# A mixture-of-experts stage whose experts are taken in the order of their token counts, with three of them held in one operand tile instead of two

## The chip, the cores and the metric

The kernel runs on one core of one Trainium2 chip. Its time is the device time of one execution in microseconds, and it is stated as the median of several runs. The five engines of a core are TensorE (PE, with its weight loads PEld), VectorE (DVE), ScalarE (ACT), GpSimd (POOL) and SyncE (SP, which here issues the DMAs).

## The reference

Two layers of a diffusion backbone with 256 latent tokens and 256 context tokens, model width 1024. The change is in the last stage, the mixture of experts of the second layer. A router picks for each of the 256 tokens two of eight experts; each expert is a SwiGLU of hidden width 3584:

```python
def _swiglu(h, w1, w3, w2):
    return (jax.nn.silu(h @ w1) * (h @ w3)) @ w2

def _moe(h, w_router, w1, w3, w2):
    logits = (h @ w_router).astype(F32)
    top_v, top_i = lax.top_k(logits, TOP_K)
    top_w = jax.nn.softmax(top_v, axis=-1)
    gates = jnp.sum(jax.nn.one_hot(top_i, N_EXPERTS, dtype=F32) * top_w[..., None], axis=-2).astype(h.dtype)
    out = jnp.zeros_like(h)
    for e in range(N_EXPERTS):
        out = out + gates[..., e:e + 1] * _swiglu(h, w1[e], w3[e], w2[e])
    return out
```

So there are 512 pairs of token and expert. Which expert gets how many depends on the data. `setup_inputs` draws all arrays from a key (`seed=0` by default) and then multiplies some of the parameters by fixed factors. The weights of the eight experts are 352 MB in single precision.

## The kernel before

**Precision.** A product of single precision is made of three products of rounded operands: x and w are each split into a high part and the remainder (`xeh`, `xel` of the tokens; `whi`, `wlo` of the weights), and `mm3` (L244) adds high by high, high by low and low by high in PSUM. ACT writes the high part of a weight tile (L215), DVE the low part (L222). A weight tile is 128 x 2048 values, 1 MB in memory.

**Routing.** `route` (L1445) makes for each half of the tokens the two choices, the gates, and in `pos1` each token's place among its expert's tokens, counted from 1 (0 where the expert is not chosen). L1491 to L1495 count the tokens of each expert and keep the greatest count in `cnt_i`.

**Experts.** `experts` (L1635) goes through the experts 0 to 7 in this order, each in four blocks of hidden columns (`FT`: three of 1024, one of 512). For a block, `up` (L1535) makes the products with w1 and w3 (PSUM tiles `eh`), `mid` (L1600) takes silu times product (`esil`), transposes it on PE (`eT`) and splits it into `ehi` and `elo`; `down` (L1551) of the block before stands between them and adds to the PSUM tiles `ey`. Per expert 42 weight tiles come in, 28 for w1 and w3 and 14 for w2.

**Gather and scatter.** `gather` (L1569) collects the tokens of two experts at once, 128 places for each: a one-hot matrix `ohr` from `pos1`, products with it (`xg`, 256 columns), an affine step on ACT (`xe`), and the split into `xeh` and `xel` on DVE. It is called ahead of expert 0 and in the third block of every second expert. `scatter` (L1620) multiplies the result by the gate row (`ye`), splits it (`yel`, on POOL except for the last expert), brings it back to token places with `ohT` (`es`) and adds it to `macc`.

**More than 128 tokens.** Behind the last expert `finish` (L1666) makes the layer norm and writes the output. Then every engine reads `cnt_i` into a register, and if the greatest count is over 128 all eight experts run once more for the places from 129 on, and `finish` too:

```python
    cv = nc.values_load(cnt_i[0:1, 0:1])
    with tc.If(cv > P):
        experts(P)
        finish()
```

**Order and buffers.** A scheduler places the instructions of each engine; within an engine they run in that order. Weight tiles land in eight buffers (`eraw`, L1521: four and one of `rp`, three of `mr`) and are split into three pairs of `whi` and `wlo` (pool `wq`, `NW` = 3). SP issues all loads in one queue, and each waits for its buffer, that is for the DVE instruction which read it last.

Of the kernel before, what the change touches and what calls it, by code (L numbers as in the profile page):

```python
# [9 lines left out]
F32 = mybir.dt.float32  # L10
# [7 lines left out]
P = 128  # L18
# [20 lines left out]
NMP = 0  # L39
NW = 3  # L40
D = 1024
# [20 lines left out]
def shape_tables():  # L62
# [40 lines left out]
    for h in (0, 16):  # L103
        for j in range(8):
# [10 lines left out]
    t["k_iota"] = np.tile(np.arange(1, 257)[None, :], (P, 1)) * 1.0  # L115
    t["k_cst"] = np.concatenate([t.pop("k_ident"), np.moveaxis(t.pop("k_cum"), 0, 1).reshape(P, -1),
                                 np.moveaxis(t.pop("k_mask"), 0, 1).reshape(P, -1), t.pop("k_bd"), t.pop("k_perm"),
                                 t.pop("k_tri"), t.pop("k_iota")], axis=1)
# [46 lines left out]
def tile_backbone(ctx: ExitStack, tc: tile.TileContext, A: dict, out: bass.AP, dbg=None, upto=99):  # L165
# [1214 lines left out]
    iot = const([P, 256], "iotk")  # L1380
    nc.sync.dma_start(iot, A["k_cst"][:, 1064:1320])
# [52 lines left out]
    cnt_i = keep([1, 1], "cnti", I32)  # L1434
# [9 lines left out]
    raws = {}  # L1444

# [47 lines left out]
    cm = until_experts([1, 1], "cmax")  # L1493
    V.tensor_reduce(cm, cps[0:1, 0:NE], axis=AX.X, op=ALU.max)
    cpy(cnt_i, cm)  # L1495
# [38 lines left out]

    def up(st, key, t):  # L1535
        e, (f0, w_) = st["e"], FT[t]
        ps = [bank("eh", "b") for _ in range(w_ // 512)]
        n = 2048 // w_
        for c0 in range(0, KC, n):
            raw = eraw(key, None).rearrange("p (c f) -> p c f", f=w_)  # L1540
            wload(raw, A[key][0, e, P * c0:P * (c0 + n), f0:f0 + w_].rearrange("(c p) f -> p c f", p=P))
            w = wsplit(raw)
            for k in range(n):
                c = c0 + k
                x = [v[:, c, st["sl"]] for v in st["x"]]
                for hf, acc in enumerate(ps):
                    sl = slice(512 * hf, 512 * hf + 512)
                    mm3(acc, x, (w[0][:, k, sl], w[1][:, k, sl]), c == 0, c == KC - 1)
        return ps

    def down(st, t):  # L1551
        e, (f0, w_) = st["e"], FT[t]
        if t == 0:
            st["y"] = [bank("ey", "a") for _ in range(2)]
        hi, lo = st["h"][t]
        for j2 in range(w_ // 256):

            raw = eraw("moe_w2", None).rearrange("p (c f) -> p c f", f=D)
            r0 = f0 + 256 * j2
            wload(raw, A["moe_w2"][0, e, r0:r0 + 256, :].rearrange("(p c) f -> p c f", c=2))  # L1560
            w = wsplit(raw)
            for c in range(2):
                i = 2 * j2 + c
                for hf in range(2):
                    sl = slice(512 * hf, 512 * hf + 512)
                    mm3(st["y"][hf], (hi[:, i], lo[:, i]), (w[0][:, c, sl], w[1][:, c, sl]),
                        t == 0 and i == 0, t == len(FT) - 1 and i == w_ // P - 1)

    def gather(e0, s0):  # L1569

        ohr = kp_.tile([P, 2, 256], F32R, name=nm("ohr"), tag="ohr", bufs=1)
        ohT = kp_.tile([P, 4, P], F32R, name=nm("ohT"), tag="ohT", bufs=2)
        for b in range(2):
            for j in range(2):
                ts(ohr[:, b, P * j:P * j + P], iot[:, s0:s0 + P], pos1[:, b, e0 + j:e0 + j + 1], ALU.is_equal)
        xeh = mp.tile([P, KC, 256], F32R, name=nm("xeh"), tag="xeh", bufs=2)
        xel = mp.tile([P, KC, 256], F32R, name=nm("xel"), tag="xel", bufs=2)
        for q in range(KC // 2):
            ps = bank("xg", "a", [P, 2, 256])
            xe = mp.tile([P, 2, 256], F32, name=nm("xe"), tag="xe", bufs=2)  # L1580
            for i in range(2):
                c = 2 * q + i
                for b in range(2):
                    sl = slice(P * c, P * c + P)
                    mm(ps[:, i], xhi[:, b, sl], ohr[:, b], b == 0 and i == 0, False, skip_group_check=True)
                    mm(ps[:, i], xlo[:, b, sl], ohr[:, b], False, b == 1 and i == 1, skip_group_check=True)
            for i in range(2):
                c = 2 * q + i
                act(xe[:, i], ps[:, i], AF.Identity, bias=kg[:, 1, c:c + 1], scale=kg[:, 0, c:c + 1])
            sl = slice(2 * q, 2 * q + 2)  # L1590
            split(xeh[:, sl], xel[:, sl], xe, "v")
        tps = bank("ohT", "a", [P, 4, P])
        for j in range(2):
            for b in range(2):
                PE.transpose(tps[:, 2 * j + b], ohr[:, b, P * j:P * j + P].bitcast(F32), ident)
# [125 lines left out]
```

## Time and profile before

| | |
|---|---|
| median of 3 runs | 1998.88 us (1998.78 to 2006.72) |
| the profiled execution | 1999.65 us, of it span 1997.9 us |
| PE busy | 96% of the span |
| DVE, ACT, POOL busy | 70%, 53%, 14% |
| DMA, mean over the span | 247 GB/s |
| first matmul of an expert; last | 995.06 us; 1976.53 us |
| DMA between 1050 and 1950 us | 362 GB/s, the 16 DMA engines 98% busy |

The experts fill the second half of the span. The profiled execution's own time stands 0.77 us over the median. The matmuls are pipelined, so PE's busy time says that it always had one under way, not how fast they followed each other; that is read from their start times. A weight tile's way is SP, DMA, ACT, DVE, PE, and each buffer goes back up the same way; so the first of these engines that can't keep up sets the pace of all.

### The profile page before, as it was taken

How to read it: one execution, taken by the hardware profiler on the slowest of the kernel's cores; microseconds unless marked ns; L12 is line 12 of the kernel's file. 1: busy time of each engine (PE TensorE's matmuls, PEld its weight loads, DVE VectorE, ACT ScalarE, POOL GpSimd, SP SyncE). 2: the span in 40 equal slices, each digit the busy share in tenths (PEclk: the TensorE clock that was granted, in tenths of full speed). 3: DMA queues.
4: the chain of work that ended last, by engine and by line, in shares of the span. 5: the costliest groups of instructions: out<-in, count | busy, mean ns of one | idle time of the engine just before them, and what ended most of it. 6: DMA issues, size and time to landing. Idle time of an engine off the chain costs nothing.

```text
span 1997.9 us, 24418 instructions
## 1 busy us (share of the span) xinstructions
PE 1923.3 (96%) x9615; PEld 1530.2 (77%) x9615; DVE 1400.3 (70%) x1457; ACT 1060.0 (53%) x1057; POOL 273.1 (14%) x235
## 2 busy tenths in 40 slices
PE   6999999899999998999899999999999999999996
PEld 3786467788888887957688888888888888888884
DVE  4653455644333446446789899989889898898986
ACT  3541234332222224325477777777776777777773
POOL 2221220250211226121000000101001010010101
PEclk9999999999999998999899999999999999999998
DMA  9515553413232434365489999999999999999992
GB/s 305 187 69 184 222 197 100 158 64 106 89 109 66 134 113 134 121 243 190 165 305 385 378 348 353 348 369 373 361 346 345 379 364 369 343 349 370 361 377 94
DMA packets 161866, 493.18 MB, mean 247 GB/s; under 512 B 12123, under 2 KB 52928, under 8 KB 141264
## 3 DMA queue, kind: packets, MB, share of 16 engines
q1 hardware_dynamic: 161744, 491.55, 68.1%
q8 instruction: 77, 1.26, 0.3%
q14 instruction: 45, 0.37, 0.1%
HBM read 486.77 MB, written 4.74 MB: 246 GB/s over the span
## 4 chain that ended last, share of the span: by engine, by line
PE 88%; DVE 6%; ACT 1%; POOL 1%; issue 1%; DVEq 0%; ACTq 0%; POOLq 0%
PE eh L234 29%; PE pf L234 17%; PE ey L234 13%; PE w L234 6%; PE wo L234 3%; DVE wlo L222 2%; PE gemv L234 2%; PE pt L234 2%; PE sm L234 2%; PE om L234 1%; PE eT L1615 1%; PE U L234 1%; PE yv L234 1%; PE oa L234 1%; POOL yel L222 1%; PE pT L1080 1%
## 5 line engine op out<-in xcount | busy, mean ns | idle before, releaser
L222 DVE TENSOR_TENSOR wlo<-moe_w,whi 128x2048 fp32r<-128x2048 f32 x336 | 769.0, 2312 | 82.5 <-ACT whi L215 81.6
L215 ACT ACTIVATE whi<-moe_w 128x2048 fp32r<-128x2048 f32 x336 | 644.8, 1921 | 208.9 <-PE eh L234 117.6
L234 PE MATMUL eh<-whi,xel 128*128 128x512 f32 x896 | 349.8, 391 | 1.1 <-DVE xel L222 1.1
L234 PE MATMUL eh<-wlo,xeh 128*128 128x512 f32 x896 | 350.0, 391 | 0.0
L234 PE MATMUL eh<-whi,xeh 128*128 128x512 f32 x896 | 319.1, 391 | 1.9 <-DVE xeh L219 1.9
L234 PE MATMUL pf<-hhi,whi 128*128 128x512 f32 (+2 forms) x560 | 210.1, 379 | 4.8 <-ACT hhi L211 2.3
L234 PE MATMUL pf<-hlo,whi 128*128 128x512 f32 (+2 forms) x560 | 211.5, 378 | 2.1 <-DVE hlo L222 2.0
L234 PE MATMUL pf<-hhi,wlo 128*128 128x512 f32 (+2 forms) x560 | 211.0, 377 | 0.1
L234 PEld LDWEIGHTS eh<-whi,xeh 128*128 128x128 f32 x896 | 168.6, 189 | 37.0 <-DVE xeh L219 2.1
L234 PEld LDWEIGHTS eh<-whi,xel 128*128 128x128 f32 x896 | 168.9, 189 | 36.5 <-DVE xel L222 1.6
L234 PEld LDWEIGHTS eh<-wlo,xeh 128*128 128x128 f32 x896 | 168.8, 188 | 35.3 <-DVE wlo L222 0.2
L234 PE MATMUL ey<-wlo,ehi 128*128 128x512 f32 x448 | 177.9, 397 | 1.3 <-DVE wlo L222 1.3
L234 PE MATMUL ey<-whi,elo 128*128 128x512 f32 x448 | 174.8, 390 | 0.6 <-DVE elo L222 0.6
L234 PE MATMUL ey<-whi,ehi 128*128 128x512 f32 x448 | 157.0, 390 | 0.5 <-ACT ehi L215 0.5
L222 POOL TENSOR_TENSOR yel<-ye,yeh 128x512 fp32r<-128x512 f32 x14 | 38.8, 2770 | 866.1 <-ACT yeh L215 859.4
L215 ACT ACTIVATE whi<-ffn_w 128x1024 fp32r<-128x1024 f32 x44 | 46.7, 1062 | 174.0 <-PE w L234 94.1
L234 PEld LDWEIGHTS pf<-hhi,whi 128*128 128x128 f32 (+1 forms) x560 | 106.2, 191 | 26.9 <-ACT hhi L211 2.6
L234 PEld LDWEIGHTS pf<-hlo,whi 128*128 128x128 f32 (+1 forms) x560 | 106.6, 190 | 24.1 <-DVE hlo L222 3.2
L234 PEld LDWEIGHTS pf<-hhi,wlo 128*128 128x128 f32 (+1 forms) x560 | 106.4, 190 | 20.2 <-issue 1.6
L222 DVE TENSOR_TENSOR wlo<-ffn_w,whi 128x1024 fp32r<-128x1024 f32 x40 | 52.7, 1318 | 73.4 <-ACT whi L215 72.6
L234 PEld LDWEIGHTS ey<-wlo,ehi 128*128 128x128 f32 x448 | 84.4, 188 | 19.8 <-DVE wlo L222 3.4
L234 PEld LDWEIGHTS ey<-whi,ehi 128*128 128x128 f32 x448 | 84.0, 188 | 18.5 <-ACT ehi L215 0.9
(345 smaller groups left out, 2774.9 us busy)
## 6 DMA issues: line engine op xcount, KB each, us to landing
moe_w<-in_moe_w_dram SPq DMA_DIRECT2D x336, 1024.0 KB
wm<-in_w_mod_dram SPq DMA_DIRECT2D x48, 1024.0 KB
ffn_w<-in_ffn_w_dram SPq DMA_DIRECT2D x22, 1024.0 KB
wi<-in_w_in_dram SPq DMA_DIRECT2D x14, 1024.0 KB
w<-in_ffn_w_dram SPq DMA_DIRECT2D x10, 1024.0 KB
wo<-in_w_out_dram SPq DMA_DIRECT2D x8, 1024.0 KB
wmla<-in_p_mla_dram SPq DMA_DIRECT2D x10, 256.0 KB
gate<-grd SPq DMA_DIRECT2D x10, 256.0 KB
```

The lines of the kernel that those rows point to most:

```text
L215: S.activation(o, i, AF.Copy)
L222: (eng or V).tensor_tensor(out=o, in0=a, in1=b, op=op)
L234: PE.matmul(o, l, r, start=start, stop=stop, **kw)
L1080: PE.transpose(pt[:, P * q:P * q + P], pr[:, P * q:P * q + P], ident)
L1615: PE.transpose(ps[:, P * i:P * i + P], s4[:, j2, c], ident)
```

## The change

- A list of slots: `CAPS` gives the places of each slot (128 or 64), `RANKS` which rank by token count it takes. Slot 0 is always expert 0 with 128 places (its key is set to -1, so it has rank 0), so that its loads need no register. The other seven are ranked by their counts; ranks 1, 2 and 3 go to the slots 1, 3 and 7, which have 64 places, the others to slots with 128.
- `order_experts` (new) works out ranks, the experts' numbers by slot (`idx_i`), places and gates by slot (`poss`, `gatess`), and `over_i`, the greatest of count minus places over all slots.
- Loads of the slots 1 to 7 take the expert's number from a register of SP (`expert_at`).
- A slot of 64 places holds the high parts of its tokens in columns 0 to 63 and the low parts in 64 to 127 of one tile. `mmx` then makes two products, with `whi` and with `wlo`; the two halves of rows are added in `mid` by a product with `fold` (two identity matrices, one above the other), which takes the place of the transposes, and after `down` by the scatter, whose one-hot matrix has the places twice.
- `gather` is called once for each slot, with 128 or 64 columns.
- Behind `finish`, the eight slots run once more, with 128 places each, if `over_i` is over 0 (before: if the greatest count was over 128).
- One more buffer for weight tiles (`NMP` = 1).

```diff
-NMP = 0
+NMP = 1
+CAPS = (128, 64, 128, 64, 128, 128, 128, 64)
+RANKS = (0, 1, 4, 2, 5, 6, 7, 3)
...
+    E0 = 0
+    def order_experts():
...
+        key, rank, cs, ov = (v[:, i] for i in range(4))
+        stt(key, cnt_f, float(NE), iot[:, 0:NE], ALU.mult, ALU.add)
+        V.memset(key[:, E0:E0 + 1], -1.0)
+        sq = [P, NE, NE]
+        tt(pm, key[:, :, None].to_broadcast(sq), key[:, None, :].to_broadcast(sq), ALU.is_gt)
+        V.tensor_reduce(rank, pm, axis=AX.X, op=ALU.add)
+        tt(pm, iot[:, 256:264, None].to_broadcast(sq), rank[:, None, :].to_broadcast(sq), ALU.is_equal)
+        tt(n8[:, 0], pm, iot[:, None, 0:NE].to_broadcast(sq), ALU.mult)
+        tt(n8[:, 1], pm, cnt_f[:, None, :].to_broadcast(sq), ALU.mult)
+        V.tensor_reduce(v[:, 2:4], n8, axis=AX.X, op=ALU.add)
+        ts(idx_i, cs[0:1], -1.0, ALU.add)
+        tt(ov, ov, iot[:, 264:272], ALU.subtract)
+        V.tensor_reduce(cs[:, 0:1], ov, axis=AX.X, op=ALU.max)
+        cpy(over_i, cs[0:1, 0:1])
+        for src, dst in ((pos1, poss), (gates, gatess)):
+            for b in range(2):
+                tt(n8[:, b], pm, src[:, b, None, :].to_broadcast(sq), ALU.mult)
+            V.tensor_reduce(dst, n8, axis=AX.X, op=ALU.add)
...
+    def mmx(acc, x, w, first, last):
+        if len(x) == 2:
+            mm3(acc, x, w, first, last)
+        else:
+            mm(acc, x[0], w[0], first, False)
+            mm(acc, x[0], w[1], False, last)
...
+        if len(st["x"]) == 1:
+            s3 = mp.tile([P, 1024], F32, name=nm("es3"), tag="es3")
+            pt = [bank("eT", "a", [P, 8, 64]) for _ in range(2)]
+            for hf in range(n // 512):
+                sh = slice(512 * hf, 512 * hf + 512)
+                for o, src, dst in ((s, p1, pt[0]), (s3, p3, pt[1])):
+                    cpy(o[:, sh], src[hf], "s")
+                    o4 = o[:, sh].rearrange("p (j q c) -> p j c q", j=2, c=2)
+                    for i in range(4):
+                        mm(dst[:, 4 * hf + i], o4[:, i // 2, i % 2], fold, hf == 0 and i == 0,
+                           hf == n // 512 - 1 and i == 3, skip_group_check=True)
+            m = n // P
+            sil = mp.tile([P, 8, 64], F32, name=nm("esl"), tag="esl")
+            act(sil[:, 0:m], pt[0][:, 0:m], AF.Silu)
+            tt(sil[:, 0:m], pt[1][:, 0:m], sil[:, 0:m], ALU.mult)
+            split(hi[:, 0:m, 0:64], hi[:, 0:m, 64:128], sil[:, 0:m])
+            st["h"][t] = (hi,)
+            return
...
+    def expert_at(s):
+        rv = nc.values_load(idx_i[0:1, s:s + 1], engines=(mybir.EngineType.SP,), min_val=0, max_val=NE - 1,
...
+        return bass.ds(rv, 1)
...
-                if t == 2 and e % 2 == 1 and e + 1 < NE:
-                    sts += gather(e + 1, s0)
+                if t == 2 and s + 1 < NE:
+                    nxt = get(s + 1)
...
-    experts(0, True)
+    experts(poss, CAPS, True)
...
-    cv = nc.values_load(cnt_i[0:1, 0:1])
-    with tc.If(cv > P):
-        experts(P)
+    cv = nc.values_load(over_i[0:1, 0:1])
+    with tc.If(cv > 0):
+        pos2 = kp_.tile([P, 2, NE], F32, name="pos2", tag="pos2")
+        for b in range(2):
+            tt(pos2[:, b], poss[:, b], iot[:, 264:272], ALU.subtract)
+        experts(pos2, (P,) * NE)
         finish()
```

**PE, two chunks of an expert's `up`**, in the second expert taken (a chunk is one 128-row piece of the weights; `eh` are the sums, `xeh` and `xel` the tokens). Before:

```order
L234 MATMUL eh_8741<-whi_8763,xeh_7858 128x512
L234 MATMUL eh_8742<-whi_8763,xeh_7858 128x512
L234 MATMUL eh_8741<-wlo_8764,xeh_7858 128x512
L234 MATMUL eh_8741<-whi_8763,xel_7859 128x512
L234 MATMUL eh_8742<-wlo_8764,xeh_7858 128x512
L234 MATMUL eh_8742<-whi_8763,xel_7859 128x512
L234 MATMUL eh_8741<-whi_8763,xeh_7858 128x512
L234 MATMUL eh_8741<-wlo_8764,xeh_7858 128x512
L234 MATMUL eh_8741<-whi_8763,xel_7859 128x512
L234 MATMUL eh_8742<-whi_8763,xeh_7858 128x512
L234 MATMUL eh_8742<-wlo_8764,xeh_7858 128x512
L234 MATMUL eh_8742<-whi_8763,xel_7859 128x512
```

Now, in slot 1, which has 64 places:

```order
L239 MATMUL eh_8814<-whi_8832,xeh_8603 128x512
L239 MATMUL eh_8815<-whi_8832,xeh_8603 128x512
L239 MATMUL eh_8814<-wlo_8833,xeh_8603 128x512
L239 MATMUL eh_8815<-wlo_8833,xeh_8603 128x512
L239 MATMUL eh_8814<-whi_8832,xeh_8603 128x512
L239 MATMUL eh_8814<-wlo_8833,xeh_8603 128x512
L239 MATMUL eh_8815<-whi_8832,xeh_8603 128x512
L239 MATMUL eh_8815<-wlo_8833,xeh_8603 128x512
```

Each pair of `whi` and `wlo` now meets one operand, `xeh`, twice where it met `xeh` twice and `xel` once.

**SP, from the loads of the first expert to those of the second.** Before:

```order
L319 DMA moe_w_1797_8693<-in_moe_w_dram 128x2048
L319 DMA moe_w_1800_8711<-in_moe_w_dram 128x2048
L319 DMA moe_w_1809_8743<-in_moe_w_dram 128x2x1024
L319 DMA moe_w_1812_8761<-in_moe_w_dram 128x2x1024
L319 DMA moe_w_1815_8779<-in_moe_w_dram 128x2x1024
```

Now:

```order
L324 DMA moe_w_1804_8784<-in_moe_w_dram 128x2048
L1698 TENSOR_LOAD idxi
L324 ISA
L324 DMA moe_w_1813_8816<-in_moe_w_dram 128x2x1024
L324 ISA
L324 DMA moe_w_1816_8830<-in_moe_w_dram 128x2x1024
L324 ISA
L324 DMA moe_w_1819_8844<-in_moe_w_dram 128x2x1024
```

The number of the expert is read into a register once (TENSOR_LOAD), and an instruction that works out the address (ISA) stands ahead of each load.

**SP, at the end of the experts**, with the last weight load, the rows for the last norm, the output and the branch. Before:

```order
L319 DMA moe_w_3039_15087<-in_moe_w_dram 128x2048
L1670 DMA lrow_15132<-in_ln_g_dram 128x1024
L1670 DMA lrow_15132<-in_ln_b_dram 128x1024
L1684 DMA out_dram<-fin_15135 128x512 x4
L1688 TENSOR_LOAD cnti
L1689 COMPARE_AND_BRANCH
L319 DMA moe_w_3074_15247<-in_moe_w_dram 128x2x1024
```

Now:

```order
L324 DMA moe_w_3071_14923<-in_moe_w_dram 128x2048
L1745 DMA lrow_14964<-in_ln_g_dram 128x1024
L1745 DMA lrow_14964<-in_ln_b_dram 128x1024
L1759 DMA out_dram<-fin_14967 128x512 x4
L1763 TENSOR_LOAD overi
L1764 COMPARE_AND_BRANCH
L1698 TENSOR_LOAD idxi
L324 ISA
L324 DMA moe_w_3102_15073<-in_moe_w_dram 128x2x1024
```

The branch stands where it stood, but reads another value; behind it the loads of a second round over the experts follow, and each takes its expert from a register.

## Rows read from the trace of the kernel before

**Rows 1.** The page: busy time, share of the span and instructions of each engine.

```profile
PE 1923.3 (96%) x9615; PEld 1530.2 (77%) x9615; DVE 1400.3 (70%) x1457; ACT 1060.0 (53%) x1057; POOL 273.1 (14%) x235
```

**Rows 2.** Busy times by stretch: the experts from 1050 to 1950 us, and a refill.

```profile
core 0: us, PE busy (x) PEld busy (x) DVE busy (x) ACT busy (x) POOL busy (x), PEclk, DMA share, GB/s
1050.00:1950.00 900.00, 896.35 (x4086) 743.96 (x4085) 813.89 (x493) 663.49 (x451) 38.79 (x14) 1.00 0.98 362
1055.00:1095.00 40.00, 40.00 (x181) 32.87 (x180) 36.37 (x22) 30.07 (x21) 0.00 (x0) 1.00 1.02 412
```

**Rows 3.** Waits from 1050 to 1950 us: who waited for whom, us in total, times, longest.

```profile
ACT whi L215 <- PE eh L234: 104.9, 137, 1.8
DVE wlo L222 <- ACT whi L215: 70.9, 127, 1.4
PE es L234 <- POOL yel L222: 3.2, 6, 0.5
...
SPq L319 <- DVE wlo L222: 751.1, 307, 4.1
```

**Rows 4.** POOL in order of time: start us, us, operation; one row per expert.

```profile
1266.39 3.19 POOL L222 TENSOR_TENSOR yel<-ye,yeh 128x512 fp32r<-128x512 f32 x1 [113.16 <-ACT yeh L215]
...
1386.88 3.19 POOL L222 TENSOR_TENSOR yel<-ye,yeh 128x512 fp32r<-128x512 f32 x1 [114.00 <-ACT yeh L215]
...
1511.75 3.19 POOL L222 TENSOR_TENSOR yel<-ye,yeh 128x512 fp32r<-128x512 f32 x1 [118.37 <-ACT yeh L215]
```

**Rows 5.** PE in order of time, within an expert: start us, us, operation.

```profile
1209.10 0.39 PE L234 MATMUL ey<-wlo,ehi 128*128 128x512 f32 x1
...
1211.14 0.39 PE L234 MATMUL ey<-whi,elo 128*128 128x512 f32 x1
```

**Rows 6.** Groups from 1050 to 1950 us: shapes, count | busy us, mean ns | idle before.

```profile
L222 DVE TENSOR_TENSOR wlo<-moe_w,whi 128x2048 fp32r<-128x2048 f32 x310 | 710.0, 2313 | 71.7 <-ACT whi L215 70.9
L215 ACT ACTIVATE whi<-moe_w 128x2048 fp32r<-128x2048 f32 x309 | 593.2, 1921 | 190.5 <-PE eh L234 104.9 <-PE ey L234 83.6 <-ACT yeh L215 0.3
L222 DVE TENSOR_TENSOR esil<-eh,esil 128x512 f32<-128x512 f32 x51 | 35.0, 691 | 12.9 <-PE eh L234 12.9
L222 DVE TENSOR_TENSOR elo<-eT,ehi 128x512 fp32r<-128x512 f32 x53 | 34.3, 683 | 0.0
L211 ACT ACTIVATE esil<-eh 128x512 f32<-128x512 f32 x51 | 30.2, 595 | 13.3 <-PE eh L234 11.2
L1615 PE MATMUL eT<-ident,esil 128*128 128x128 f32 x208 | 30.0, 281 | 0.0
L231 DVE SCALAR_TENSOR_TENSOR macc<-es,gates,macc 128x512 f32<-128x512 f32 x28 | 19.6, 739 | 0.0
L222 DVE TENSOR_TENSOR ye<-ey,grow 128x512 f32<-128x512 f32 x14 | 9.0, 686 | 0.0
L222 DVE TENSOR_TENSOR xel<-xe,xeh 128x512 fp32r<-128x512 f32 x12 | 8.3, 688 | 0.1
L219 DVE CAST xeh<-xe 128x512 fp32r<-128x512 f32 x12 | 5.1, 424 | 1.4 <-ACT xe L211 1.4
```

**Rows 7.** The start of the experts in order of time, PE and DVE.

```profile
995.06 0.50 PE L234 MATMUL eh<-whi,xeh 128*128 128x512 f32 x1 [1.89 <-DVE xeh L219]
...
985.08 0.15 DVE L1494 TENSOR_REDUCE cmax<-count 1x1 f32<-1x8 f32 x1
```

**Rows 8.** The end in order of time, PE and SP.

```profile
1976.53 0.39 PE L234 MATMUL ey<-whi,elo 128*128 128x512 f32 x1
...
1987.89 4.24 SPq L1684 DMA_DIRECT2D out_dram<-fin  x4
```

**Rows 9.** Groups of the whole span, PE: a plain f32 product of 64 columns.

```profile
L234 PE MATMUL om<-vm,pT 128*128 128x64 f32 x320 | 42.0, 270 | 0.0
```

**Rows 10.** Reading the flag and branching: count, duration ns min/median/max, first and last start.

```profile
L1689 SPq COMPARE_BRANCH  x1: 50/50/50, 1993.3 to 1993.3; - x1
...
L1688 SPq TENSOR_LOAD <-cnti x1: 732/732/732, 1992.5 to 1992.5; - x1
```

More of the change, by code (lines that the diff above doesn't have):

```diff
@@ L1592, in gather @@
[L1592 to L1595, printed above, removed]
+            for j in range(P // cap):
+                ts(ohr[:, b, cap * j:cap * j + cap], iot[:, 0:cap], pos[:, b], ALU.is_equal)
+        xeh = mp.tile([P, KC, P], F32R, name=nm("xeh"), tag="xeh", bufs=2)
+        if cap == P:
+            xel = mp.tile([P, KC, P], F32R, name=nm("xel"), tag="xel", bufs=2)
+            x = (xeh, xel)
+        else:
+            xel = xeh[:, :, cap:]
+            x = (xeh,)
@@ L1596, in gather @@
+        tps = bank("ohT", "a", [P, 2, P])
+        for b in range(2):
+            PE.transpose(tps[:, b], ohr[:, b].bitcast(F32), ident)
         cpy(ohT, tps)
-        return [{"e": e0 + j, "x": (xeh, xel), "sl": slice(P * j, P * j + P), "ohT": ohT[:, 2 * j:2 * j + 2], "h": {}}
-                for j in range(2)]
+        return {"s": s, "e": e, "x": x, "ohT": ohT, "h": {}}
     def mid(st, t, p1, p3):
@@ L1632, in scatter, with experts, get @@
                 mm(ps, st["ohT"][:, b], lo, False, True)
-                stt(macc[:, b, sl], ps, gates[:, b, st["e"]:st["e"] + 1], macc[:, b, sl], ALU.mult, ALU.add)
-    def experts(s0, residual=False):
-        sts = gather(0, s0)
-        side[0] = NSM if residual else 0
+                stt(macc[:, b, sl], ps, gatess[:, b, st["s"]:st["s"] + 1], macc[:, b, sl], ALU.mult, ALU.add)
+    def expert_at(s):
+        rv = nc.values_load(idx_i[0:1, s:s + 1], engines=(mybir.EngineType.SP,), min_val=0, max_val=NE - 1,
+                            skip_runtime_bounds_check_because="a place in a list of eight, made of compares")
+        return bass.ds(rv, 1)
+    def experts(pos, caps, first=False):
+        def get(s):
+            if first and s == 0:
+                return gather(0, slice(E0, E0 + 1), pos1[:, :, E0:E0 + 1], caps[0])
+            return gather(s, expert_at(s), pos[:, :, s:s + 1], caps[s])
+        nxt = get(0)
+        if first:
+            order_experts()
+        side[0] = NSM if first else 0
         pend = None
         nt = len(FT)
-        for e in range(NE):
-            st = sts[e]
+        for s in range(NE):
+            st = nxt
             for t in range(nt):
```

78 lines of the change are left out of this document (40 added, 38 removed).

## The prediction

> **What bounds the kernel now.** I read first the page's busy times: PE is busy for 96% of the span [rows 1]. That is no proof, as matmuls overlap, so the second view is the busy times by stretch: over the experts, from 1050 to 1950 us, PE is busy for 896 of 900 us, DVE for 814, ACT for 663, and the DMA engines are 98% busy at 362 GB/s [rows 2]. Three resources look nearly full. The third view, the waits, tells who leads: SP waits 751 us for DVE to free weight buffers, DVE 71 us for ACT, ACT 105 us for PE, and PE for next to nothing, 3.2 us on POOL [rows 3]. The waits climb the weights' way backwards and end at PE; nobody waits for a DMA. So PE sets the pace, and the DMA moves what PE has used. But the others are close behind, and their prices per expert decide how much a lighter PE can bring.
>
> **The pace per expert.** POOL splits each expert's result once, so its starts are a clock: 120.5 us for an expert without a gather, 124.9 us with one [rows 4]; a gather of two experts costs 4.4 us. PE alone explains it. Ten matmuls of 512 columns in a row, of which the first and the last are shown, take nine steps of together 2.04 us, 0.227 us each [rows 5]; an expert has 168 triples, 504 x 0.227 = 114.4 us, with 28 transposes of 0.144 us (30.0 us over 208) and 8 matmuls of the scatter 120.2 us [rows 6]. The sum of the stage, 8 x 120.5 + 3 x 4.4 = 977.2 us, leaves 4.7 of the 981.9 us from the first `eh` at 995.06 to the end of the last `ey` at 1976.92 [rows 7, 8] for the start.
>
> **Does the light form fit the data?** Of a change that branches on token counts this comes first. The reference, evaluated on its own inputs (seed 0), gives the experts 0 to 7 in this order 53, 70, 50, 67, 69, 74, 38 and 91 tokens. Before, the greatest, 91, is under 128, so the second round is skipped. Now expert 0 is set into slot 0, and the other seven are ranked: 38, 50, 67, 69, 70, 74, 91. Ranks 1, 2 and 3 have 64 places, and rank 3 has 67 tokens. Three are left over, `over_i` is 3, the branch is not skipped, and all eight experts run once more at 128 places for three tokens. (Had expert 0 been ranked with the rest, 38, 50 and 53 would have fitted.) The smallest gap between the second and the third logit of any token is 0.0015, so rounding doesn't move the counts. The order of SP shows what follows the branch: a whole further round of loads. This decides the forecast, whatever the light form is worth.
>
> **The first round: what it removes.** In the slots with 64 places 168 matmuls of 0.227 us go, 38 us each on PE. 28 transposes become 56 products with `fold`; of that form (128x64, plain f32) the trace has 320 at 0.131 us [rows 9], 7.3 us against 4.0. PE would need about 336 x 0.227 + 7.3 + 2 + a gather's 3 = 88 us. What is late next? DVE still splits 42 weight tiles: 42 x 2.29 (710.0 us over 310) = 96.2 us; products and low parts shrink to 3.5 x (0.69 + 0.68) = 4.8; `macc` 4 x 0.74, `ye` 2 x 0.69, the next gather's `xeh` and `xel` 2 x (0.42 + 0.69): together 107.6 us [rows 6]. ACT has 42 x 1.92 + 14 copies of 0.6 us and under 10 us more, 99 us. DMA: 42 tiles of 1.0486 MB, 44.04 MB; in the 40 us in which it refilled the buffers it moved 412 GB/s [rows 2], which is 106.9 us. So a light expert is bounded by DVE at 107.6 with DMA beside it; with two limits that close I take 111 us, between 107.6 and the 120.5 of today, near the first because PE is nearest to its own sum today (120.2 of 120.5). The gain is not 38 but about 10 us each.
>
> [...]
>
> **What it adds.** Gathers: one per slot. One costs between 2.2 us (half of a pair's, if columns count) and 4.4 us (as many instructions as a pair's); 3.2 us, the middle, as no row is nearer. In the light slots DVE hides it; in the five others PE pays. `order_experts`: about 20 small DVE instructions at the start; the reduction of the counts took 0.15 us [rows 7], the largest at most the 0.7 us of a 128x512 one: 3 to 14 us, of which the start, where DVE waits for first tiles, hides some. I take 3. The last slot is a light one: its chain of copies, `fold`, silu, product and split stands ahead of the last `down`: 1 us more (0 to 3). SP: a register load (0.73 us of that kind [rows 10]) seven times, and an address instruction ahead of each of 294 loads; SP waits 751 of 900 us [rows 3], and that wait hides them up to some 2 us per load. The ninth buffer shortens no wait on PE's side: nothing. Five experts at 120.5 + 3.2 and three at 111 make 951.5 us against 977.2; less 4 us that is **22 us gained in the first round**. Its ends: 41 with 107.6 and 2.2, minus 22 if the light ones stay at 120.5, gathers cost 4.4 and the rest its full price.
>
> **The second round.** SP has its first free place after the last output's issue, 1987.89 + 4.24 = 1992.1 us [rows 8]; reading the flag and branching took it until 1993.3 [rows 10]. Then the expert's number, the first load at about 1994.5, its landing some 4 us later (2.5 us for 1 MB at 412 GB/s, more as eight loads share the engines), 1.9 on ACT and 2.3 on DVE, and the split of `xeh` behind that on DVE: the first `eh` at 2004, 27 us behind the end of the last `ey`. The norm, PE's gather and the other engines' branches lie within it. If the first load lands ahead of all others it is 24, if eight land together (20 us) 43. The round itself: 8 x 120.5 + 7 x 3.2 + 4.7 for the start = 991 us; 984 to 1003 with the gather's ends and a dearer start. The end behind the last `ey`, 21.0 us today, stays.
>
> **The sum**, in the profiled execution's time: 1976.9 - 22 + 27 + 991 + 21.0 = 2993.9 us of span, and 1.75 us between its span and its time (1999.65): 2995.7. The median of the runs stands 0.8 us lower: **2995 us**, 50% slower.
>
> **Rivals.**
> *The second round is not taken* (the change does what it says, and this one ends on the other side). The point is whether the third smallest of the seven ranked experts has at most 64 tokens in what is fed in. Then the branch is skipped and 1998.9 - 22 = 1977 us remain, 1.1% faster. For it: before, the same kind of flag skipped the round, and the nearest count misses by three tokens. Against: the counts above are of the reference's own inputs. Chance 0.13, for inputs that come out other than mine.
> *The light experts gain nothing.* The DMA engines are 98% busy at 362 GB/s over the whole stage [rows 2]; if that is what they sustain, 44.04 MB take 121.7 us. The first round is then 618.5 + 365 + 4 = 987.6, 10 us longer than today, and the time 3027 us. Against it: in all that stage SP waited for buffers, not DVE for data. Chance 0.14.
> *SP becomes the bound.* Loads with an address from a register have no row. If one costs over the 2.87 us (120.5/42) in which PE uses a tile, SP sets the pace of 15 experts; at 3.5 us it is 630 x 0.63 = 397 us more, 3390 us. Against: the register load, the nearest, takes 0.73 us. Chance 0.04.
>
> **How the numbers follow.** The forecast has 0.69. The range takes in the second rival and the ends of the first round's gain, the gap and the round, not all at their worst at once: 2955 to 3040 us. Left out are the first and the last rival and some 0.03 of tails. A measurement of this kernel can tell about 0.5% from no change, 10 us: faster 0.12 and the same 0.01 (the first rival, the latter with a gain near nothing), slower 0.87.
>
> **What would show it.** The trace of the changed kernel should show 16 experts: about twice the instructions of `whi` and `wlo` (672), twice the output's four DMAs, and a stretch without `eh` of some 27 us near 1980 us. In the slots 1, 3 and 7 the time between two splits of POOL should be near 111 us, with DVE over 95% busy, PE near 80% and DMA near 400 GB/s; in the second round near 124 us, with PE full. If PE is full in the light slots, the price of `fold` or of a pair is wrong; if DMA is at 360 GB/s and DVE waits for data, the second rival is right; if SP no longer waits for buffers, the third. A span under 2000 us would mean that the counts are not mine, and then the light slots alone decide.

## The result: the second round is run, and the first gains nothing

The changed kernel takes **3033.85 us** (median of 4 runs, 3023.14 to 3035.52) against 1999.59 us (4 runs, 1998.78 to 2006.72) of the kernel before on the same chip: a ratio of 1.515, 95% interval 1.510 to 1.520. That lies inside the range of the forecast, 39 us above its number. Executions of the kernel before differ by up to 17 us with the clock that TensorE is granted (1995 us at a mean of 0.986 of the full clock, 2012 us at 0.978; one of ten of c_fit below, at 0.84, took 2137 us and is left out of its ratio), so the experiments below are told by their ratio to runs of the kernel before on the same chip.

The page of the changed kernel (busy us, share of the span, instructions; then two groups with count, busy us and mean ns, and idle before them):

```profile
span 3031.5 us, 37213 instructions
PE 2909.9 (96%) x14083; PEld 2319.3 (77%) x14083; DVE 2282.9 (75%) x2038; ACT 1801.7 (59%) x1642; POOL 315.1 (10%) x253
...
L227 DVE TENSOR_TENSOR wlo<-moe_w,whi 128x2048 fp32r<-128x2048 f32 x672 | 1533.8, 2308 | 198.7 <-ACT whi L220 197.3
L220 ACT ACTIVATE whi<-moe_w 128x2048 fp32r<-128x2048 f32 x672 | 1283.2, 1917 | 392.5 <-PE eh L239 188.3
```

672 weight tiles are split, 16 experts' worth: the second round ran, as forecast, and a tile's prices didn't change (2308 and 1917 ns; [rows 6] had 2313 and 1921). The time between two splits of POOL shows the pace of the slots, as [rows 4] did before (start us, us, operation; the first of the two halves, for the slots 0 to 4 and then for the slots 0 to 2 of the second round):

```profile
1160.98 3.34 POOL L227 TENSOR_TENSOR yel<-ye,yeh 128x512 fp32r<-128x512 f32 x1 [169.51 <-ACT yeh L220]
...
1273.68 3.17 POOL L227 TENSOR_TENSOR yel<-ye,yeh 128x512 fp32r<-128x512 f32 x1 [106.06 <-ACT yeh L220]
...
1399.49 3.17 POOL L227 TENSOR_TENSOR yel<-ye,yeh 128x512 fp32r<-128x512 f32 x1 [119.32 <-ACT yeh L220]
...
1517.80 3.17 POOL L227 TENSOR_TENSOR yel<-ye,yeh 128x512 fp32r<-128x512 f32 x1 [112.90 <-ACT yeh L220]
1642.91 3.19 POOL L227 TENSOR_TENSOR yel<-ye,yeh 128x512 fp32r<-128x512 f32 x1 [118.62 <-ACT yeh L220]
...
2162.51 3.19 POOL L227 TENSOR_TENSOR yel<-ye,yeh 128x512 fp32r<-128x512 f32 x1 [158.39 <-ACT yeh L220]
...
2287.63 3.20 POOL L227 TENSOR_TENSOR yel<-ye,yeh 128x512 fp32r<-128x512 f32 x1 [118.61 <-ACT yeh L220]
2412.76 3.20 POOL L227 TENSOR_TENSOR yel<-ye,yeh 128x512 fp32r<-128x512 f32 x1 [118.64 <-ACT yeh L220]
```

Slot 1 (light) took 112.7 us, slot 2 (full) 125.8, slot 3 (light) 118.3, slot 4 125.1; each interval has a gather in it. The full slots of the second round take 125.1 too. These intervals don't part the slots quite: a slot's split stands behind the first block of the next slot's `up`, so each interval holds 8 of the next slot's 42 weight tiles. Counted from the first `whi` of a slot to the first of the next, the slots 1 to 4 took 114.4, 125.3, 117.8 and 124.7 us. Now the gap between the rounds, in order of time on PE, SP, ACT and PE again:

```profile
1988.68 0.40 PE L239 MATMUL ey<-wlo,ehi 128*128 128x512 f32 x1
...
2005.73 32.65 SPq L324 DMA_DIRECT2D moe_w<-in_moe_w_dram  x18
...
2010.86 1.91 ACT L220 ACTIVATE whi<-moe_w 128x2048 fp32r<-128x2048 f32 x1 [10.45 <-DMA moe_w<-in_moe_w_dram]
...
2015.49 0.79 PE L239 MATMUL eh<-whi,xeh 128*128 128x512 f32 x1 [3.78 <-DVE xeh L224]
```

From the end of the last `ey` (1989.08) to the first `eh` 26.4 us pass; 27 were forecast. Set against the steps of the forecast:

| stretch | before | forecast | after | after minus forecast |
|---|---|---|---|---|
| up to the first `eh` | 995.1 | 995.1 | 1007.3 | +12.2 |
| first round (first `eh` to the end of the last `ey`) | 981.9 | 959.9 | 981.8 | +21.9 |
| gap | - | 27 | 26.4 | -0.6 |
| second round | - | 991 | 997.9 | +6.9 |
| end behind the last `ey` | 21.0 | 21.0 | 18.1 | -2.9 |

The rows add up to 37.5 of the 37.6 us between 2995.7 and the profiled 3033.35. What was to be found out: whether those three tokens are the cause of the thousand, why the first round gained nothing, and where the 12 us ahead of the experts come from, in which the change has no work.

### The profile page after: what moved, and what is told of

It is laid out like the page before. It is cut to its first block, busy times and chain, and to the rows that moved or that the text cites. A ratio compares the mean times of both kernels' runs of the same rounds, so it can differ in the third digit from the quotient of the medians.

```text
span 3031.5 us, 37213 instructions
## 1 busy us (share of the span) xinstructions
PE 2909.9 (96%) x14083; PEld 2319.3 (77%) x14083; DVE 2282.9 (75%) x2038; ACT 1801.7 (59%) x1642; POOL 315.1 (10%) x253
## 4 chain that ended last, share of the span: by engine, by line
PE 50%; DVE 6%; issue 2%; POOL 2%; ACT 1%; DMA 0%; DVEq 0%; SPq 0%; ACTq 0%; POOLq 0%
PE eh L239 31%; PE ey L239 15%; DVE wlo L227 5%; POOL yel L227 2%; PE xg L239 1%; PE eT L1677 1%; ACT whi L220 1%; PE eT L239 1%; PE es L239 1%; DVE ye L227 0%; ACT yeh L220 0%; DVE esil L227 0%; DVE macc L236 0%; DMA moe_w<-in_moe_w_dram 0%; POOL fin L227 0%
## 5 line engine op out<-in xcount | busy, mean ns | idle before, releaser
L227 DVE TENSOR_TENSOR wlo<-moe_w,whi 128x2048 fp32r<-128x2048 f32 x672 | 1533.8, 2308 | 198.7 <-ACT whi L220 197.3
L220 ACT ACTIVATE whi<-moe_w 128x2048 fp32r<-128x2048 f32 x672 | 1283.2, 1917 | 392.5 <-PE eh L239 188.3
L239 PE MATMUL eh<-wlo,xeh 128*128 128x512 f32 x1792 | 697.7, 396 | 18.6 <-DVE wlo L227 17.0
L239 PE MATMUL eh<-whi,xeh 128*128 128x512 f32 x1792 | 642.4, 393 | 6.4 <-DVE xeh L224 5.8
L239 PE MATMUL eh<-whi,xel 128*128 128x512 f32 x1456 | 570.6, 392 | 0.0
L239 PEld LDWEIGHTS eh<-wlo,xeh 128*128 128x128 f32 x1792 | 335.6, 189 | 106.7 <-DVE wlo L227 38.5
L239 PEld LDWEIGHTS eh<-whi,xeh 128*128 128x128 f32 x1792 | 338.0, 189 | 78.9 <-DVE xeh L224 6.4
L239 PE MATMUL ey<-wlo,ehi 128*128 128x512 f32 x896 | 357.5, 406 | 7.6 <-DVE wlo L227 7.1
L239 PE MATMUL ey<-whi,ehi 128*128 128x512 f32 x896 | 321.9, 398 | 6.8 <-DVE ehi L227 6.3
L239 PEld LDWEIGHTS ey<-wlo,ehi 128*128 128x128 f32 x896 | 168.5, 190 | 51.6 <-DVE wlo L227 17.1
L239 PEld LDWEIGHTS ey<-whi,elo 128*128 128x128 f32 x728 | 137.5, 189 | 29.8 <-DVE elo L227 0.9
L239 PEld LDWEIGHTS pf<-hhi,wlo 128*128 128x128 f32 (+1 forms) x560 | 107.6, 192 | 22.3 <-issue 1.6
```

Source lines behind the costliest of these rows:

```text
L220: S.activation(o, i, AF.Copy)
L227: (eng or V).tensor_tensor(out=o, in0=a, in1=b, op=op)
L239: PE.matmul(o, l, r, start=start, stop=stop, **kw)
```

## The experiments: what runs, and for what

**Another expert in slot 0 (c_fit), and the same without light slots (d_full).** With expert 1 (70 tokens) in slot 0 the three smallest of the rest have 38, 50 and 53 tokens, and all fit.

```diff
-    E0 = 0
+    E0 = 1
```
```diff
-CAPS = (128, 64, 128, 64, 128, 128, 128, 64)
+CAPS = (128,) * 8
```

> The changed kernel with expert 1 (70 tokens) in slot 0 instead of expert 0 (53): the three smallest of the ranked ones then have 38, 50 and 53 tokens, all within 64 places, and the second round isn't run. The same instructions in the same order up to the flag. If the forecast's cause of the 1000 us is right, they go whole: 3033.4 - 26.4 (gap) - 997.9 (second round) = 2009 us, so slower than before by 0.5%, as the first round gained nothing and 12 us were lost ahead of it. By the forecast's own sizes for the first round: 1977 us. If the time stays near 3033, the flag doesn't hang on those three tokens.

> The kernel of the run with expert 1 first, but with 128 places in all eight slots: no light form, still a gather, a register and an address for each slot, no second round. It parts the light form's worth from the cost of one gather per slot. Theory: the light slots took 112.7, 118.3 and 95.6 us where full ones take 125.1, 125.1 and 99.3, so this kernel is 22.9 us slower than the one with light slots, about 2032 us, and 33 us slower than before: 12 ahead of the experts, 18 for four gathers more of 4.6 us each, 3 at start and end. Rival 2 of the forecast (the light form gains nothing): the same time as with light slots within 3 us. The forecast's sizes: 10 us per light slot, 28 more in all.

c_fit: 2011.7 us, 1.0034 of the kernel before (1.0014 to 1.0054). One number in the code takes the second round away, and its time goes whole; the order of the instructions up to the branch is the same. So the flag did hang on those three tokens. d_full: 2027.8 us, 1.0104 (1.0071 to 1.0136). Its trace, beside that of c_fit, has a first round of 999.0 us against 978.9: the three light slots are worth 20.1 us together, near the 22.9 expected (the medians of the runs stand 16 us apart); that they gain nothing (rival 2) is out. But the rest of the change (a gather for each slot, the registers, the ordering, and a longer step of `ey`, of which more below) cost 17.1 us (999.0 against the 981.9 of before), so the two nearly cancel.

## The experiments: the 12 us ahead of the experts

**The kernel before again (a_same); with the wide table alone (b_wide); c_fit with a cell put back (h_addr, and timed as h_again).** The change widens `iotk` by 320 bytes and drops the cell `cmax`, so tiles of the first stages stand elsewhere.

```diff
-    iot = const([P, 256], "iotk")
+    iot = const([P, 336], "iotk")
```
```diff
+    cm = until_experts([1, 1], "cmax")
+    V.tensor_reduce(cm, cps[0:1, 0:NE], axis=AX.X, op=ALU.max)
```

> The kernel before once more, nothing changed: how far a time, and the 995.1 us up to the first matmul of the experts, differ from run to run. In the changed kernel that stretch took 1007.3 us, 12.2 us more, though the change doesn't touch the work in it. If runs or chips differ by so much, this one shows a first matmul anywhere from 995 to 1007 and times that spread by 12 us. If not: 995 within 1 us, and 1999 us.

> The kernel before with the table iotk widened from 256 to 336 columns, as in the changed kernel, and nothing else; the experts are those of before. Theory: the wider tile shifts the buffers behind it and the order of some 30 instructions ahead of the experts, and that is where the 12.2 us come from: first matmul of the experts at 1007 us, 2011 us in all. Rival: the 12 us belong to something else of the change (the buffers of the experts, the code of twice the length): first matmul at 995, 1999 us.

> The kernel with expert 1 first, with the unused cell cmax of the kernel before put back (and the one reduction that fills it): in the stretch ahead of the experts all tiles then stand at the addresses of the kernel with the wide table, 32 bytes further for one pool than in the changed kernel, and the order is the same. In that stretch the steps of PE's matmuls are 0.2290 us in the kernel before, 0.2302 with the wide table and 0.2332 in the changed one. If the addresses set them: 0.2302 and a first matmul of the experts near 996 to 1003 us. If not: 0.2332 and 1008.

> The kernel with expert 1 first and the cell cmax put back, timed again: its one run was 1996.3 us, that without the cell 2011.7 (median of ten). Of the kernel before the runs lie between 1995 and 2012 us, those near 1998 with a granted clock of 0.985, those near 2007 with 0.979, so a single run doesn't tell addresses from clock. If 32 bytes of address set the time: 1996 to 2000 us in nearly all runs, clock 0.982 or more. If it was the run: 2007 to 2012 us in most.

a_same gave 0.9992 (0.9975 to 1.001), b_wide 1.0004 (0.9984 to 1.0024), with the first `eh` at 998.5 and 995.8 us: the wide table is not it. h_addr ran in 1996.3 us, and h_again, the same kernel timed six times, in 1999.1 us, 0.9975 (0.9959 to 0.9991), against the 1.0034 of c_fit: by the medians the cell is worth about 12 us. The first `eh` came at 998.2 and 1000.7 us, in c_fit at 1009.0, and the first round took 975.4 and 974.9 us for 978.9. Two things show in the rows. Busy times by stretch in the dense middle of the first stages, of the kernel before, the changed one and h_again (columns as in [rows 2]; the number behind x is the matmuls):

```profile
450.00:750.00 300.00, 300.00 (x1311) 245.91 (x1310) 126.45 (x147) 74.77 (x88) 55.28 (x34) 1.00 0.33 104
...
450.00:750.00 300.00, 300.00 (x1290) 241.89 (x1289) 120.99 (x137) 76.18 (x90) 52.34 (x32) 1.00 0.30 96
...
450.00:750.00 300.00, 300.00 (x1304) 244.98 (x1304) 123.31 (x138) 76.11 (x90) 52.27 (x32) 1.00 0.30 98
```

PE never pauses (300.00 of 300 us busy) and the clock is granted in full (1.00) in all three, yet 1311, 1290 and 1304 matmuls start: 0.2288, 0.2326 and 0.2301 us a step. From the first product with `wo` to the last `pf` the changed kernel took 6.1 us more than before (540.2 against 534.1). The number goes with the kernel and not with the execution: a_same has 1311 too, c_fit 1288, h_addr 1305. PE's instructions and their order are the same in c_fit and h_again there; by the kernels' layout the tiles of one pool stand 32 bytes apart. The traces hold no addresses, so the place of the tiles is what is left over as the cause, and not shown by itself; how it would get into PE's step, no run here shows.

The other half is the clock that was granted before that. p_pairs and s_order, two kernels of the next section, have the same instructions and places up to the experts, and yet their first `eh` came at 998.3 and 1013.9 us. Their first two stretches (PEclk is the third number from the end of a row):

```profile
20.00:310.00 290.00, 276.83 (x1688) 187.14 (x1687) 156.57 (x290) 103.84 (x182) 66.35 (x73) 1.00 0.54 194
310.00:450.00 140.00, 134.08 (x698) 109.92 (x697) 77.16 (x138) 55.07 (x107) 43.20 (x32) 0.99 0.27 91
...
20.00:310.00 290.00, 280.39 (x1669) 191.17 (x1670) 150.72 (x280) 99.67 (x175) 66.31 (x74) 0.96 0.52 187
310.00:450.00 140.00, 130.38 (x649) 104.15 (x650) 77.93 (x143) 57.07 (x113) 43.58 (x32) 0.94 0.30 100
```

The same instructions, two executions: 1.00 and 0.99 of the full clock in one, 0.96 and 0.94 in the other. The changed kernel's profile has 0.98 and 0.95 there, that of before 0.99 and 0.98, and by the first product with `wo` it was 6.3 us behind (320.9 against 314.6). So by the traces about half of the 12 us goes with the longer step, and the rest can't be told from what two executions of the same instructions differ by: u_best (next section) has the cell and the 1305 matmuls, and yet its first `eh` came at 1007.1 us, with the clock at 0.98 and 0.94. Whether the cell has a part in the clock too (0.977 in most runs of c_fit, 0.980 in most of h_again) is open.

## The experiments: why a light slot took 113 to 118 us

**What the trace says.** Slot 3 of the changed kernel, by busy times (columns as in [rows 2]) and by waits (who for whom, us, times, longest):

```profile
1404.00:1517.00 113.00, 105.52 (x510) 83.62 (x509) 102.70 (x64) 88.26 (x69) 0.90 (x1) 1.00 0.98 375
```
```profile
PEld eh L239 <- DVE wlo L227: 11.9, 15, 1.7
DVE wlo L227 <- ACT whi L220: 8.4, 10, 1.5
ACT whi L220 <- PE eh L239: 5.9, 7, 1.6
...
ACT esl L216 <- PE eT L239: 4.2, 2, 2.1
ACT esil L220 <- PE eh L239: 4.1, 2, 2.9
ACT es L220 <- PE eh L239: 4.1, 2, 2.3
```

PE waits for DVE now, as forecast, but DVE is not full: 102.7 of 113 us. It waits for ACT, and ACT for PE, both for a free pair of split tiles and in its three new kinds of instruction, which read PE's sums. In order of time, ACT and then DVE:

```profile
1418.07 1.91 ACT L220 ACTIVATE whi<-moe_w 128x2048 fp32r<-128x2048 f32 x1
1422.28 0.60 ACT L220 ACTIVATE es<-eh 128x512 f32<-128x512 f32 x1 [2.30 <-PE eh L239]
1422.77 1.90 ACT L220 ACTIVATE whi<-moe_w 128x2048 fp32r<-128x2048 f32 x1
...
1424.71 2.29 DVE L227 TENSOR_TENSOR wlo<-moe_w,whi 128x2048 fp32r<-128x2048 f32 x1 [1.52 <-ACT whi L220]
```

The copy `es` stands in ACT's order where its sum is not there yet; ACT is idle for 2.30 us ahead of it, the next `whi` starts behind it, and DVE runs dry for 1.52 us. Two things could hold ACT up, then: its place in the order, or that there are only three pairs, so that the `whi` behind the copy would have had to wait for the same tile anyway.

**Without the low parts (m_nolo): is it the DMA?** In the light slots `wsplit` makes `whi` alone, and both products read it.

```diff
+        if light:
+            cpy(hi, raw, "s")
+            return hi, hi
```

> The kernel with expert 1 first, without the low parts of the weights in the light slots: DVE's wlo is left out there and the second pass reads whi again, so that PE, ACT and the loads stay as they are. DVE is then nearly idle in light slots. If DMA were what holds them (44.04 MB at 362 GB/s are 121.7 us, at the 384 of the light slots 114.7), they stay at 113 to 118 us. If the chain of ACT, DVE and PE does, they fall to what ACT needs, about 100 us with 42 x 1.92 + 14 x 0.6 + gather, and DMA shows what it can move: over 420 GB/s.

1975.6 us, in one run; the slots 1 and 3 took 105.0 and 108.5 us in place of 112.7 and 118.3. Slot 3:

```profile
1387.00:1495.00 108.00, 104.37 (x520) 86.10 (x518) 31.31 (x31) 89.57 (x71) 2.30 (x2) 1.00 1.02 404
```

The loads went at 404 GB/s, and no wait for one shows there; so 362 GB/s is what the full slots asked for, not what the DMA can do, and rival 2 has lost its cause too. The slots did not fall to ACT's 100 us: with DVE out of it, ACT and PE still wait for each other (`whi` 4.1 us for PE's `eh`, PE's weight loads 3.0 us for `whi`).

**Four pairs (n_four).** One pair more of `whi` and `wlo`, two load buffers less.

```diff
-NMR = 3
+NMR = 2
-NMP = 1
-NW = 3
+NMP = 0
+NW = 4
```

> The kernel with expert 1 first, with four pairs of split weight tiles (whi, wlo) instead of three, paid for with two of the nine load buffers. In its light slots ACT copies eh in between the splits and waits for PE there (2.3 and 2.9 us at a time), then DVE waits for whi and PE for wlo. Theory: the chain from PE's release of a tile over ACT (1.9 us) and DVE (2.3) back to PE is too long for three pairs when PE needs only 1.8 us of products per tile and ACT and DVE have other work in between; a fourth pair covers it, the light slots go from 112.7, 118.3 and 94.5 us toward DVE's own 103, some 20 us less in all: 1991 us. Rival 2 of the forecast (DMA is the limit in light slots): no gain, or a loss from fewer load buffers: 2011 us or more. The full slots stay at 125 by both.

1.0001 (0.9985 to 1.0017): a miss. Slot 3 still took 118.1 us (and slot 1 118.0, the last 95.5). Its waits in that slot:

```profile
DVE wlo L227 <- ACT whi L220: 7.8, 6, 1.9
ACT esil L220 <- PE eh L239: 5.7, 3, 2.9
...
ACT esl L216 <- PE eT L239: 4.2, 2, 2.1
ACT es L220 <- PE eh L239: 4.1, 2, 2.3
...
ACT whi L220 <- PE eh L239: 0.4, 1, 0.4
```

The wait for a free pair is gone (5.9 to 0.4 us), those in the copies are not, and DVE waits about as long (7.8 us for 8.4). That speaks for the order. No engine waited for a load in that slot, so there it wasn't the two load buffers less that hid a gain. The first round took 972.0 us where c_fit had 978.9, but its first `eh` came 6.9 us later; from the first split of POOL to the end of the last `ey` it took 830.1 us for 825.3.

**Four pairs and ACT's copies later (r_order); three pairs and the copies later (s_order); gathers for two slots (p_pairs).** In r_order each copy and silu must stand in ACT's order behind (`behind`) the third or fourth `whi` that follows the tile it waits for:

```diff
-                for o, src, dst in ((s, p1, pt[0]), (s3, p3, pt[1])):
-                    cpy(o[:, sh], src[hf], "s")
+                for o, src, dst, w in ((s, p1, pt[0], w1), (s3, p3, pt[1], w3)):
+                    behind(S.activation(o[:, sh], src[hf], AF.Copy), w)
```

p_pairs gathers (1, 2), (3, 4) and (5, 6) together, with slot 5 light in place of 7:

```diff
-CAPS = (128, 64, 128, 64, 128, 128, 128, 64)
+CAPS = (128, 64, 128, 64, 128, 64, 128, 128)
...
+            ss = (s, s + 1) if first and s < 7 else (s,)
+            return gather(*[(i, expert_at(i), pos[:, :, i:i + 1], caps[i]) for i in ss])
```

s_order is p_pairs with the copies behind the third `whi`.

> The kernel with four pairs of split tiles, and in the light slots ACT's copies of eh and its silu put behind the third or fourth whi that follows the tile they wait for, instead of the first or second; nothing else moves but what the scheduler does around it. With four pairs alone the light slots stayed at 118.0, 118.1 and 95.5 us: ACT no longer waited for a free pair (0.4 us in place of 6.0), but still 16 us for PE in its copies, and DVE 7.8 us for whi. Theory: ACT takes its work in order, and a copy that waits for PE holds the next whi up; behind a later whi it finds its data ready. Then DVE's waits for whi go, and slot 3 falls from 118.1 to about 109 us (DVE's own 106 and a little), 20 us less in all: 1987 us. Rival: the order of ACT is not what DVE waits on, slot 3 stays at 118 and the time near 2007.

> The kernel with expert 1 first, with gathers for two slots at a time (192 columns: a light one and a full one), the first and the last slot alone: five gathers instead of eight; the light slots are 1, 3 and 5, the last is a full one; eight load buffers. The forecast took 3.2 us for one gather of a single slot, by the trace it is as dear as a pair's (full slots 125.1 us, of which 120.5 are products, 1.0 a longer step of the matmuls and 3.4 to 4.6 the gather). Theory: three gathers less in the sum, 10 to 14 us: about 2000 us, full slots without a gather at 121.5. If a gather cost by its columns, nothing is won: 2011.

> The kernel with gathers for two slots, and the same shift of ACT's copies, with three pairs of split tiles: copies stand behind the third whi that follows the tile they wait for, which for three pairs is the one that needs that tile's buffer, so that a copy never waits longer than the whi ahead of it has. Theory: each of the four blocks of a light slot gives back what the copies held up, up to the 8.4 us that DVE waits for whi in a slot; slots 3 and 5 fall from 114.5 to 107 to 111 us, 10 to 20 us in all: 1971 to 1981 us. Rival (with three pairs the buffers hold the next whi up all the same): 114 and 1991.

r_order: 1980.0 us, 0.9859 (0.9832 to 0.9887). Against n_four the first round went from 972.0 to 953.2 us, 18.8 where 20 were expected, slot 3 from 118.1 to 114.5 where 109 was expected. Busy times and waits of that slot:

```profile
1393.00:1507.00 114.00, 107.96 (x524) 86.49 (x524) 104.96 (x66) 90.08 (x73) 3.98 (x3) 1.00 1.01 395
```
```profile
DVE wlo L227 <- ACT whi L517: 2.6, 2, 1.9
...
ACT esl L1669 <- PE eT L239: 2.1, 1, 2.1
...
ACT es L1662 <- PE eh L239: 0.8, 1, 0.8
```

DVE's wait went from 7.8 to 2.6 us. p_pairs: 1991.4 us, 0.9919 (0.9891 to 0.9947), first round 959.2 us, 19.7 less than c_fit for three gathers fewer; more than the 10 to 14 expected, but 4.1 of it lie ahead of the first split; that the third light slot is no longer the last one may have a part in it, and was not tried by itself. s_order: 1988.9 us, 0.99 (0.9869 to 0.9931), first round 958.5 us against 959.2: a miss, the rival was right. Its waits in slot 3, 114.5 us long as in p_pairs:

```profile
ACT whi L517 <- PE eh L239: 9.9, 14, 1.6
...
DVE esl L227 <- PE eT L239: 6.5, 3, 3.1
...
DVE wlo L227 <- ACT whi L517: 2.7, 5, 0.9
```

The copies `es` and `esil` wait no more, and DVE's wait for `whi` fell from the 8.4 us of p_pairs to 2.7; but ACT now waits 9.9 us for a free pair (5.9 in p_pairs), and DVE's product `esl` waits 6.5 us (0.4) for the products with `fold`, which stand behind the later copies. The wait has moved and not gone. So neither four pairs alone nor the order alone brought anything, and both together did: from the first split to the last `ey`, r_order is 18.9 us shorter than n_four and 14.1 shorter than c_fit. The order alone was tried with the gathers for two slots, four pairs alone without them, so this isn't one table of four runs; but u_best below, which adds the fourth pair to the gathers and the order (with most copies one `whi` later, and the cell), is 21.8 us shorter there than s_order. Either one by itself is enough to hold the chain of ACT, DVE and PE.

**All of it (u_best).** The edits of r_order and p_pairs and the cell, and two to make room:

```diff
-            s3 = mp.tile([P, 1024], F32, name=nm("es3"), tag="es3")
+            s3 = mp.tile([P, 8, P], F32R, name=nm("es3"), tag="elo").bitcast(F32).rearrange("p a b -> p (a b)")
...
-            xe = mp.tile([P, 2, 256], F32, name=nm("xe"), tag="xe", bufs=2)
+            xe = mp.tile([P, 2, 256], F32, name=nm("xe"), tag="xe", bufs=1)
```

> All that helped, together: expert 1 first, so that the light form fits these inputs and the second round stays away; gathers for two slots at a time; four pairs of split tiles with ACT's copies behind the third or fourth whi (seven load buffers, and es3 in the space of elo); the cell cmax put back. From the single runs: the gathers took 16 us off the first round (975.4 to 959.2), the four pairs with the order 19 (972.0 to 953.2); if they add, first matmul of the experts near 999, first round near 941, tail 20.5: 1962 us, 0.978 of before. If the two overlap (both shorten the same waits of the light slots), the better of them alone: 1980 us, 0.986.

**1957.4 us, 0.9763 (0.974 to 0.9787)** of the kernel before: faster than both kernels. The first round took 930.9 us, and slot 3 ran from 1378.58 to 1485.90, 107.3 us (start us, us, operation; below it busy times and two waits of that slot):

```profile
1378.58 2.33 POOL L227 TENSOR_TENSOR yel<-ye,yeh 128x512 fp32r<-128x512 f32 x1 [114.58 <-ACT yeh L220]
...
1485.90 3.17 POOL L227 TENSOR_TENSOR yel<-ye,yeh 128x512 fp32r<-128x512 f32 x1 [101.69 <-ACT yeh L220]
```
```profile
1379.00:1486.00 107.00, 102.59 (x487) 82.20 (x486) 101.97 (x59) 87.78 (x65) 4.38 (x3) 1.00 1.02 404
```
```profile
ACT whi L517 <- DMA moe_w<-in_moe_w_dram: 3.3, 6, 0.7
...
DVE wlo L227 <- ACT whi L517: 2.5, 3, 1.7
```

The other two light slots took 106.4 and 107.4 us (104.6 and 104.0 for the slots 3 and 5 from first `whi` to first `whi`). DVE is busy for 102 of 107 us, near the 107.6 that the forecast had worked out for it; 2.2 of those were for a gather, and the light slots have none here. At 404 GB/s the first waits for a load appear, with seven load buffers; m_nolo, with nine, had none at the same rate, so these waits don't show that the DMA's limit (106.9 us by the forecast) is reached. That expert 1 stands in slot 0 fits these inputs; with other counts a second round may still be run.

## Why the prediction was right, and its steps one by one

**The number** lies 39 us under the measured one, and the range holds it by 6 us. It reaches that far because it takes in rival 2, whose cause didn't hold, and 12 of the 39 us come from a stretch in which the forecast had nothing; that the range held was in part luck. That a second round is run, and what it costs, was not.

**The second round** decided, as the forecast said: counting the tokens of the reference's own inputs, in the order that the new code gives them, was worth 1000 us of the answer, and c_fit shows it. The gap was 26.4 us for 27. The chain in it was also the one named: flag, first load, `whi`, `wlo`, `xeh`, first `eh`.

**A full slot** was forecast at 123.7 us (120.5 and 3.2 for the gather) and took 125.1; over the six intervals between the splits of the second round that is 8.6 us, and its start and end together were 1.7 us shorter than forecast: the +6.9. The gather was not far off. Part of the rest is PE's step. In order of time, eight steps of `ey` in a full slot of the changed kernel:

```profile
1701.86 0.39 PE L239 MATMUL ey<-whi,elo 128*128 128x512 f32 x1
...
1703.72 0.39 PE L239 MATMUL ey<-whi,elo 128*128 128x512 f32 x1
```

1.86 us for eight is 0.2325 us a step, where [rows 5] had 0.227; the steps of `eh` stayed at 0.227. Why `ey` steps longer, no run shows. An expert has 168 products of `ey`: 0.9 us. That leaves 3.7 us for a gather, within the forecast's 2.2 to 4.4 and above the middle that it took: half the columns cost more than half as much.

**A light slot** is where the forecast failed in size, and the failed step is the sentence that adds 3 us to DVE's sum for "two limits that close" because "PE is nearest to its own sum today". PE reached its sum before with three pairs of tiles, and with one kind of instruction in ACT's order that read its sums `eh`, the silu, which waited 11.2 us in 900 for them [rows 6]. The change put three kinds there that read PE's sums, and they waited 12.4 us in slot 3 alone. So the light slots took 112.7 and 118.3 us in place of 111, and the last one gained 3.7 us in place of 9.5 (95.6 against 99.3 from the last split to the last `ey`). Those are 1.7, 7.3 and 5.8 us; with 1.4 to 2.1 us in each of four full slots (6.6) they make 21.4 of the 21.9 us of the table. (By the first `whi` of each slot the light ones took 114.4 and 117.8 us; the sum is the same.) DVE's sum itself was near right: in u_best a light slot took 106.4 to 107.4 us, with DVE busy for 102. Of the signs that the forecast named, DVE was busy for 91% of slot 3 and not over 95, PE for 93% and not some 80, and the DMA moved 375 GB/s and not 400. One price in PE's sum was wrong: `fold` makes 112 records of 64 columns in slot 3 (56 on `es`, 56 on `esil`), not 56: two for each product of the code; 16 in a row took 1.99 us in c_fit. With 112 at 0.124 us PE's sum is an estimated 95 us in place of 88, still under DVE's.

**Ahead of the experts** the forecast had nothing, and 12.2 us came. It argued from the work, and the work didn't change; the step of PE in the same products and the granted clock did. The forecast's term that failed is this nothing; about half of it is the step (6.1 us), and what sets the step and the clock stays open.

**The end** was 2.9 us shorter than the 21.0 of before, and the extra 1 us forecast for the last slot's chain can't be seen apart. In the sum of the first round's gain, the lower end doesn't come out: 5 x 124.9 + 3 x 120.5 + 17 us is 1003, against 977.2 a loss of 26 and not of 22.

**The rivals.** That the second round isn't taken is out by the 672 tiles. That the light slots gain nothing gave the nearest number (3027 us), for a reason that didn't hold: the first round did come out flat, but the light slots were worth 20.1 us (d_full against c_fit), and the DMA moved 404 GB/s when it was asked to, for 107 us. That SP becomes the bound is out: it still waited 84.9 us for DVE in slot 3, and reading the expert's number took 0.27 us (median of 15).

## What to carry to other kernels

Where a change branches on data, work out from the inputs which way the branch goes before any instruction is priced; here one expert more or less in the ranking was worth 1000 us. When the engine that sets the pace is made lighter, the next bound need not be the next engine's busy sum; here it was the chain between them: look for instructions that wait for the lightened engine in the order of an engine ahead of it, and for the number of buffers, and change both, since either alone can hide the whole gain (nothing apart, 14 to 22 us together). Before a difference in a stretch without changed work is explained, compare two executions of one program there.

## What the runs showed of the hardware

- PE's step in one unbroken run of 128x512 products at the full clock was 0.2288 us (1311 in 300 us in both of before and a_same), 0.2301 (1304, h_again) or 0.2326 (1290, the changed kernel), by kernel and not by execution, and went from 0.2329 (1288, c_fit) to 0.2301 when one cell was put back that moves the tiles of a pool by 32 bytes in the layout, with PE's instructions unchanged.
- The same instructions were granted 1.00 and 0.96 of the full clock between 20 and 310 us in two executions (p_pairs and s_order), with 15.6 us between them at the first `eh`.
- One core loaded 404 GB/s for 107 us (u_best) and for 108 us (m_nolo), the 16 DMA engines full (a share of 1.02); with seven load buffers (u_best) ACT waited 3.3 us for data there, in six waits, with nine (m_nolo) no wait for data shows.
- Around a branch taken at run time 26.4 us passed from the end of the last `ey` to the first `eh`, nearly all of it the scatter, the norm, the first load and its split; from reading the flag (2004.5) to the first load's issue (2005.7) it was 1.2 us.
